# A two-layer decoder trunk on one core: the SSM preparation cut into pieces, and the first output block placed among the last attention products

## The chip, the cores and the metric

The program runs on one core of one Trainium2 chip. A core has TensorE (PE: matmuls; PEld is its weight load), VectorE (DVE), ScalarE (ACT), GpSimd (POOL) and SyncE (SP, which here issues most DMAs). The metric is the device time of one execution in microseconds (us), and lower is better. Several runs are timed and the median is taken.

## The reference, cut to what matters

Two layers work on a residual of 1024 tokens by 1024 channels. Layer 0 mixes tokens by attention, layer 1 by a state-space recurrence (S5) beside a short convolution; each mixer is followed by an MLP (1024 to 4096 to 1024, squared ReLU) and a gated per-layer embedding (PLE).

```
for i in range(2):
    hn = rms_norm(h, norm_mix[i])
    y = attention_mixer(hn, ...) if i == 0 else recurrent_conv_mixer(hn, ...)   # each ends in y @ w_out
    h = h + y
    h = h + square(relu(rms_norm(h, norm_mlp[i]) @ w_mlp_in[i])) @ w_mlp_out[i]
    h = h + (p[i] @ w_ple_proj[i]) * sigmoid(rms_norm(h, norm_ple[i]) @ w_ple_gate[i])
return rms_norm(h, norm_final)
```

The attention has 8 groups of 128 channels (4 differential heads, 4 pairs of dilated-window heads), so `y` is 8 blocks of 128 channels. The recurrence of layer 1 needs tables that depend on weights alone (powers of the complex decay, rotations, small products): they can be made at any time before layer 1, and this is called the preparation here.

## The kernel before, in words

**Products.** Activations lie transposed, channels on partitions, tokens (1024, two halves of 512) along the free dimension. Every f32 operand is split into a high part (ACT, `hi`, L76) and a low part (DVE, `lo`, L79, or `wtile`, L89), and a product is three matmuls in a row, high x high, low x high, high x low (`mm3`, L95 to L97). A weight block of 128 output channels is one `wtile`: a 512 KB DMA on SP's queue into `wr` (2 buffers), ACT's `wh`, then `wl` by DVE (by POOL during the attention); `wh` and `wl` have 3 buffers. `blocks` (L273 on) runs the output blocks of a projection: the first two or three share a loop over the 8 input blocks, then each block has 48 matmuls, two times 8 x 3, and a result bank is emptied by `out`.

**Order.** TensorE executes in the order in which the program is written. On the other engines the instructions are put in order by a planner at build time: of those that it takes to be ready it issues the one that the program names first. Tiles wait for the release of the tile whose memory or buffer they take over.

**Attention** (`at_run`, L1655 on). The order on TensorE is written by a small model of the engines with four lanes: `s` (scores), `t` (transposes of the weights), `pv` (products with v) and `u` (scaling and output). A list `fill` of projections (q, k, v and part of the PLE) is fed in between, in steps of three matmuls, while a lane has nothing due. When one list entry nears its end, `prime` starts the next one, which issues its weight DMAs. `s` has 128 tasks, four for each of 8 x 4 steps (group i, quarter of the queries). The last list entry is the q and k projection of group 7. `y_out` (L2022 on) writes each quarter of a `y` block to HBM.

**Output projection of layer 0** (`out_proj`, L328 on) loads the 8 blocks of `y` from HBM into the memory of the attention's input (`y_load`, L322), in order of SP's queue, and runs `blocks` with the first two output blocks together.

**MLP up of layer 0** (`mlp_up_plain`, L356 on). 32 blocks; `out(m, n, ps)` scales a bank, and after the second half applies ReLU and square and for odd m combines and stores (`z_out`). The preparation `s5_prep` is a generator that `out` advances at nine blocks (m = 1, 5, 9, ..., 27): the first time all of the tables and the first of 8 quads, then one quad (`s5_quad`) each time; a quad's part on TensorE (`later`) is emitted at the next call. The tiles of `out` lie in a pool `cu` on the left side of SBUF, ahead of the preparation's pool. The MLP down (`mlp_down`) then opens its pool `dn` on the left, over `cu`.

**Output projection of layer 1** (`out_proj_halves`, L409 on) runs the left token half, then the right half; while the right half's blocks m = 1 and 2 run, `out` also normalizes and splits four blocks each of the left half for the MLP that follows.

Of the kernel before, what the change touches and what calls it, by code (L numbers as in the profile page):

```python
# [65 lines left out]
class Trunk:  # L66
# [95 lines left out]
    def run(self):  # L162
        tc, nc, A = self.tc, self.nc, self.A
        pool = tc.tile_pool
        with pool(name="w", bufs=1, side=LEFT) as self.wp, \
# [11 lines left out]
            for l in range(2):  # L177
                if l == 0:
                    self.attention(xp)
                with pool(name=f"md{l}", bufs=6, space=PSUM, reuse_waits="tile") as self.mx, ExitStack() as rs:  # L180
# [4 lines left out]
                    if l == 0:  # L185
                        with pool(name=f"xu{l}", bufs=1, side=RIGHT, reuse_waits="tile") as xu:
                            hp = hs.enter_context(pool(name=f"h{l}", bufs=1, side=RIGHT, reuse_waits="tile"))
                            sp = self.ss.enter_context(pool(name=f"st{l}", bufs=1, side=RIGHT, reuse_waits="tile"))
                            xs, st = self.out_proj(l, xp, hp, xu, sp)
                            nxt.close()  # L190
                            with pool(name=f"cu{l}", bufs=1, side=LEFT, reuse_waits="tile") as cu:
                                first = self.mlp_up_plain(l, xs, st, cu, xu, hs)
# [135 lines left out]
    def out_proj(self, l, xp, hp, xq, sp):  # L328
        nc, A = self.nc, self.A
        ws = []  # L330
        if l:
            ws = [self.wtile(A["w_out"][l * KB + j]) for j in range(3)]
            order = [4, 5, 6, 7, 0, 1, 2, 3]
        else:
            order = list(range(KB))
            self.ys = {}
        ys = self.ys
        for k in order:
            if k not in ys:
                self.y_load(xp, k)  # L340
# [12 lines left out]
        self.blocks(A["w_out"][l * KB : (l + 1) * KB], ys, KB, order, out, 2 if l == 0 else 3, None if l == 0 else 4, ws)  # L353
        return xs, st

    def mlp_up_plain(self, l, xs, st, cu, xu, hs):  # L356
# [5 lines left out]
        def out(m, n, ps):  # L362
            if not r:
                r.append(self.rstd_full(st, xu, cu))
                self.ss.close()
                hs.close()
            s = slice(n * H, n * H + H)
# [14 lines left out]
        with self.tc.tile_pool(name=f"s0{l}", bufs=1, side=LEFT, reuse_waits="tile") as self.s0:  # L382
# [26 lines left out]
    def out_proj_halves(self, l, xp, hp, sp, xa, X):  # L409
# [35 lines left out]
        for s in (lt, rt):  # L445
            for m in range(3 if s is lt else 0, KB):
# [514 lines left out]
    def s5_prep(self):  # L961
# [4 lines left out]
        with tc.tile_pool(name="prep", bufs=1, side=LEFT, reuse_waits="tile") as pr:  # L966
# [16 lines left out]
            self.pexp(dt, ld, tmp)  # L983
            x = tmp()
            v.tensor_tensor(x, lr, dt, ALU.mult)
            self.pexp(mag, x, tmp)
            x = tmp()
            v.tensor_tensor(x, li, dt, ALU.mult)
            self.sincos(sn, cs, x, tmp)

# [19 lines left out]
            for t in range(8):  # L1010
                for j in range(2):
                    nc.scalar.copy(rv[j][:, t * G : (t + 1) * G], w(j, 7 - t))

# [14 lines left out]
            v.tensor_tensor(ci, ci, den, ALU.mult)  # L1028

# [16 lines left out]
            pend = None  # L1046
            for q in range(8):
                if pend:
# [3 lines left out]
            pend()  # L1052
# [11 lines left out]
    def s5_quad(self, q, pr, pw, rv, cr, ci, rot, sgn, nsgn):  # L1064
# [21 lines left out]

        def outer(out, tab, nt, X1, X2):
# [9 lines left out]
        outer(Gt, rv, 8, bb1, bb2)  # L1097
        CA = big("CA", 576)
        outer(CA, pw, 9, C1, C2)
        ca4 = CA.rearrange("p (g t c) -> p g t c", g=4, c=16)  # L1100
        cc = big("cc")
        nc.scalar.copy(cc.rearrange("p (g t c) -> p g t c", g=4, c=16), ca4[:, :, 1:9, :])
        self.spill(pr, q, 4, cc)

# [4 lines left out]
        for j in range(7):  # L1109
# [9 lines left out]
            v.tensor_tensor(s3[:, :, hi], s3[:, :, hi], m, ALU.add)  # L1119
        v.tensor_scalar(st, st, sgn, None, ALU.mult)  # L1120
# [3 lines left out]
        def later():  # L1124
            ps = self.bank()
            for g in range(4):
                nc.tensor.transpose(ps[:, g * P : g * P + P], Gt[:, g * P : g * P + P], self.ident)
            self.spill(pr, q, 2, ps)
            kp = self.bank()
            for g in range(4):  # L1130
                nc.tensor.matmul(kp[0:16, g * P : g * P + P], bb1[:, g * 16 : g * 16 + 16], ca4[:, g, 0:8, :], start=True, stop=True)
            M = big("M")
            v.memset(M, 0.0)
            kt = big("kt")[0:16]
            nc.scalar.copy(kt, kp[0:16, :])
            k4 = kt.rearrange("p (g t c) -> p g t c", g=4, c=16)
            di = pr.tile([16, 64], F32, name="di", tag="di", bufs=1)
            v.tensor_tensor(g4(di), self.ident[0:16, 0:16].unsqueeze(1).to_broadcast([16, 4, 16]),
                            self.s5_dT[:, gs].unsqueeze(2).to_broadcast([16, 4, 16]), ALU.mult)
            v.tensor_tensor(k4[:, :, 0, :], k4[:, :, 0, :], g4(di), ALU.add)  # L1140
            m4 = M.rearrange("p (g t c) -> p g t c", g=4, c=16)
            for t in range(8):
                nc.sync.dma_start(m4[t * 16 : t * 16 + 16, :, t:8, :], k4[:, :, 0 : 8 - t, :])
            self.spill(pr, q, 0, M)
        return later
# [290 lines left out]
    def attention(self, xp):  # L1436
        tc, nc, A = self.tc, self.nc, self.A
        with tc.tile_pool(name="at", bufs=1, side=RIGHT) as self.ap, \
             tc.tile_pool(name="sps", bufs=3, space=PSUM) as self.sp, \
             tc.tile_pool(name="tps", bufs=1, space=PSUM) as self.tp:  # L1440
            self.o2, self.on = None, 0
            v0 = self.at_start(xp)
# [131 lines left out]


# [79 lines left out]
    def at_run(self, v0):  # L1655
# [3 lines left out]
        fill = [("v", 0)]  # L1659
        for i in range(1, 8):  # L1660
            fill += [("qk", i)] + ([("v", i // 2)] if i % 2 == 0 else []) + late.get(i, [])
        made = {"qk": self.qk, "v": self.vproj, "pp": self.ple_proj}
# [4 lines left out]
        def may(f):  # L1667
            if f[0] == "v":
# [3 lines left out]
        def prime(n):  # L1672

            if n < len(fill) and n not in gens and (fill[n][0] != "pp" or may(fill[n])):
# [347 lines left out]
    def y_out(self, st, y):  # L2022
# [6 lines left out]
        s = slice(qp * 256, qp * 256 + 256)  # L2029
        nc.sync.dma_start(self.y_d[i][0][:, s], yh.bitcast(F32))  # L2030
# [76 lines left out]
```

## Time and profile before

| | |
|---|---|
| median of 3 runs | 2575.11 us (2574.72 to 2578.71) |
| profiled execution, its own time | 2579.28 us |
| its span, first to last instruction | 2577.5 us |
| mean granted TensorE clock | 0.985 of full |
| PE busy | 2486.7 us (96%) |
| DVE busy | 1726.0 us (67%) |
| ACT busy | 1082.6 us (42%) |
| POOL busy | 131.3 us (5%) |

A profile is one execution. Times in its rows are counted from the span's start. In a timeline row the numbers are start, length, engine, line, operation, output <- inputs, shape and count, and in brackets how long the engine was idle before it and what ended that. The granted clock has two levels, full and half (2.4 and 1.2 GHz).

### The profile page before, as it was taken

Reading aid. Unit: us, or ns where it says so; the run is one execution under the profiler, and the core shown is the slowest. Engines: PE = TensorE matmul, PEld = TensorE weight load, DVE = VectorE, ACT = ScalarE, POOL = GpSimd, SP = SyncE. Lnnn points to the kernel's source line nnn. Section 1 sums busy time; section 2 is a strip of 40 time slices with the busy share of each in tenths; the row PEclk is TensorE's granted clock in tenths of the full one; section 3 lists DMA queues with packets and bytes.
Section 4 is the critical chain, followed back from the end, with each engine's and each line's share of the span. In section 5 each row is a group of like instructions: output and inputs, shape, how many; then the busy total and the mean of one; then the engine's idle time right before and its main releaser. Section 6 shows DMA issues by size and latency. Waiting matters only on the chain.

```text
span 2577.5 us, 33019 instructions
## 1 busy us (share of the span) xinstructions
PE 2486.7 (96%) x12104; PEld 2057.1 (80%) x12104; DVE 1726.0 (67%) x3189; ACT 1082.6 (42%) x1615; POOL 131.3 (5%) x128
## 2 busy tenths in 40 slices
PE   8999999979899999899999999999899999999998
PEld 6888898968687877688887897887688887888877
DVE  6776756554766776356776768665786664568776
ACT  5554555542333333343344432333554444333445
POOL 1111111000000000000000000000000000000000
PEclk9999999989999999999999999999999999999999
DMA  5443524264254555677853656354353447677552
GB/s 175 111 131 97 150 63 118 61 198 154 85 180 164 197 190 193 270 239 242 282 191 134 212 171 194 131 187 132 139 196 135 152 170 297 235 243 280 202 183 97
DMA packets 184754, 449.82 MB, mean 175 GB/s; under 512 B 24848, under 2 KB 56848, under 8 KB 184592
## 3 DMA queue, kind: packets, MB, share of 16 engines
q1 hardware_dynamic: 155904, 371.94, 43.8%
q0 software_dynamic: 12800, 46.14, 4.6%
q10 hardware_dynamic: 15888, 29.63, 3.1%
q8 instruction: 95, 1.56, 0.3%
q14 instruction: 67, 0.55, 0.1%
HBM read 297.55 MB, written 123.73 MB: 163 GB/s over the span
## 4 chain that ended last, share of the span: by engine, by line
PE 85%; DVE 8%; ACT 2%; issue 2%; DMA 1%; SPq 0%; DVEq 0%; ACTq 0%
PE mm L95 26%; PE mm L97 26%; PE mm L96 26%; PE tp L1927 2%; PE S L1894 1%; PE S L1895 1%; PE o L1952 1%; PE o L1951 1%; DVE zl L79 1%; DVE p L1897 1%; PE S L2019 1%; DVE wl L89 0%; DVE h L465 0%; DVE tl L79 0%; DVE p L1916 0%
## 5 line engine op out<-in xcount | busy, mean ns | idle before, releaser
L97 PE MATMUL mm<-xh,wl 128*128 128x512 f32 (+1 forms) x1504 | 583.9, 388 | 13.4 <-DVE st L1108 8.7
L95 PE MATMUL mm<-xh,wh 128*128 128x512 f32 (+1 forms) x1504 | 589.9, 392 | 0.3 <-ACT wh L76 0.3
L96 PE MATMUL mm<-xl,wh 128*128 128x512 f32 (+1 forms) x1504 | 580.8, 386 | 1.6 <-DVE xl L155 1.6
L95 PE MATMUL mm<-zh,wh 128*128 128x512 f32 x880 | 350.2, 398 | 8.5 <-ACT zh L76 8.5
L96 PE MATMUL mm<-zl,wh 128*128 128x512 f32 x880 | 350.1, 398 | 1.7 <-DVE zl L79 1.7
L97 PE MATMUL mm<-zh,wl 128*128 128x512 f32 x880 | 349.8, 397 | 0.0
L97 PEld LDWEIGHTS mm<-xh,wl 128*128 128x128 f32 x1504 | 284.5, 189 | 78.2 <-DVE st L1108 9.1
L96 PEld LDWEIGHTS mm<-xl,wh 128*128 128x128 f32 x1504 | 284.7, 189 | 61.4 <-DVE xl L155 2.0
L95 PEld LDWEIGHTS mm<-xh,wh 128*128 128x128 f32 x1504 | 284.6, 189 | 59.8 <-ACT sph L76 1.5
L76 ACT ACTIVATE wh<-wr 128x1024 fp32r<-128x1024 f32 (+1 forms) x137 | 143.8, 1052 | 446.1 <-PE mm L96 356.1
L95 PEld LDWEIGHTS mm<-zh,wh 128*128 128x128 f32 x880 | 166.4, 189 | 49.9 <-ACT zh L76 9.3
L96 PEld LDWEIGHTS mm<-zl,wh 128*128 128x128 f32 x880 | 166.4, 189 | 43.0 <-DVE zl L79 2.5
L97 PEld LDWEIGHTS mm<-zh,wl 128*128 128x128 f32 x880 | 166.3, 189 | 40.5
L76 ACT ACTIVATE wh<-raw 128x1024 fp32r<-128x1024 f32 x78 | 82.7, 1060 | 239.9 <-issue 117.0
L79 DVE TENSOR_TENSOR wl<-raw,wh 128x1024 fp32r<-128x1024 f32 x78 | 95.4, 1223 | 100.3 <-ACT wh L76 100.2
L89 DVE TENSOR_TENSOR wl<-wr,wh 128x1024 fp32r<-128x1024 f32 x98 | 119.6, 1222 | 59.6 <-ACT wh L76 59.3
L1902 ACT ACTIVATE p<-p,m 128x128 f32<-128x128 f32 (+7 forms) x128 | 99.1, 774 | 96.6 <-DVE m L1897 95.5
L79 DVE TENSOR_TENSOR zl<-zr,zh 128x1024 fp32r<-128x1024 f32 x110 | 134.1, 1219 | 2.4 <-ACT zh L76 2.2
L76 ACT ACTIVATE zh<-zr 128x1024 fp32r<-128x1024 f32 x110 | 115.0, 1045 | 0.7 <-DMA zr<-oa 0.7
L95 PE MATMUL mm<-wh,xh 128*128 128x256 f32 x384 | 112.6, 293 | 2.1 <-DVE v L1651 1.4
L97 PE MATMUL mm<-wh,xl 128*128 128x256 f32 x384 | 109.7, 286 | 0.0
L96 PE MATMUL mm<-wl,xh 128*128 128x256 f32 x384 | 109.6, 285 | 0.0
(680 smaller groups left out, 4476.2 us busy)
## 6 DMA issues: line engine op xcount, KB each, us to landing
raw<-w_m SPq DMA_DIRECT2D x158, 512.0 KB, 5.8
wr<-w_m SPq DMA_DIRECT2D x69, 512.0 KB, 4.1
ot<-tt POOLq DMA_DIRECT2D x64, 512.0 KB, 5.0
zr<-ot SPq DMA_DIRECT2D x64, 512.0 KB, 4.9
ob<-z ACTq DMA_DIRECT2D x32, 512.0 KB, 4.6
zr<-ob SPq DMA_DIRECT2D x32, 512.0 KB, 4.2
s<-s SPq DMA_DIRECT2D x64, 256.0 KB, 5.0
wr<-w_out SPq DMA_DIRECT2D x24, 512.0 KB, 3.5
```

Of the source, the lines that this page charges most:

```text
L76: self.nc.scalar.activation(out, in_, AF.Copy, scale=scale)
L79: self.nc.vector.tensor_tensor(out, full, hi.bitcast(F32), ALU.subtract)
L89: self.weng.tensor_tensor(l, raw, h.bitcast(F32), ALU.subtract)
L95: mm(ps, L[0], R[0], start=first, stop=False)
L96: mm(ps, L[0], R[1], start=False, stop=False)
L97: mm(ps, L[1], R[0], start=False, stop=last)
L1894: nc.tensor.matmul(S, qh, qk["k"][c][:, k], start=True, stop=False)
L1895: nc.tensor.matmul(S, ql, qk["k"][c][:, k], start=False, stop=True)
L1897: nc.vector.tensor_tensor_reduce(pt[:, k], S, self.tab[:, T - w + k.start : T - w + k.stop], -0.125, m, ALU.add, ALU.min, m2)
L1902: nc.scalar.activation(pt[:, :w], pt[:, :w], AF.Exp, bias=m, scale=-1.0, accum_out=den)
L1927: nc.tensor.transpose(tps[:, off + n * P : off + n * P + P], maps[j][:, kb * P : kb * P + P], self.ident)
L1951: nc.tensor.matmul(oq, vv, th[:, q], start=first, stop=False)
```

## The change: what it does

1. **Preparation in pieces.** `s5_prep` and `s5_quad` yield 6 times in the tables and 9 times in each quad, and `later` becomes a straight continuation of its quad. `out` of `mlp_up_plain` advances the generator once after the first half and twice after the second half of every block from m = 1, so three pieces per block.
2. **Pools of the MLP up.** `cu` is opened on the right side of SBUF, where the output projection's `h` and statistics lay, after these are closed. The four temporaries of the norm go into the pool `s0` on the left.
3. **First output block as filler.** A new list entry `("op",)` follows the q and k projection of group 7. `op_start` loads the block's weights and `y` blocks 0 to 5, then gives 12 steps of three matmuls into two banks. It may be primed once `y_out` was emitted for groups 0 to 5; its steps may run once 10 or fewer `s` tasks are left, and only when no lane is due. `out_proj` loads `y` 6 and 7, runs output blocks 1 and 2 over `y` 0 to 5, then all three blocks over `y` 6 and `y` 7, empties six banks and goes on with blocks 3 to 7.
4. **Layer 1.** The normalizing and splitting of the left half is spread over the right half's m = 1 to 4, two blocks each.

```diff
@@ out_proj
+        for k in (6, 7):
+            self.y_load(xp, k)
...
+        self.bn = 2
+        ws = [self.op[0]] + [self.wtile(src[m]) for m in (1, 2)]
+        jobs = [(m, n, self.op[1][n] if m == 0 else self.bank()) for m in range(3) for n in range(2)]
+        for part in (range(6), (6,), (7,)):
+            for m, n, b in jobs:
+                if m or part[0]:
+                    for k in part:
+                        self.mm3(b, self.cols(ws[m])(k), [y[:, n * H : n * H + H] for y in ys[k]], k == 0, k == KB - 1)
+        for m, n, b in jobs:
+            out(m, n, b)
+        self.blocks(src[3:], ys, KB - 3, list(range(KB)), lambda m, n, b: out(m + 3, n, b), 1)
@@ mlp_up_plain
-                r.append(self.rstd_full(st, xu, cu))
+                r.append(self.rstd_full(st, xu, self.s0))
                 self.ss.close()
                 hs.close()
+                r.append(cs.enter_context(self.tc.tile_pool(name=f"cu{l}", bufs=1, side=RIGHT, reuse_waits="tile")))
...
-                if m in (1, 5, 9, 12, 16, 19, 22, 25, 27):
+            if m:
+                for _ in range(1 + n):
                     next(prep, None)
@@ out_proj_halves
-                if s is rt and m in (1, 2):
-                    for k in range(m * 4 - 4, m * 4):
+                if s is rt and m in (1, 2, 3, 4):
+                    for k in range(m * 2 - 2, m * 2):
                         self.norm_half(l, h, st, k, lt)
-                        X[m, k % 4] = self.split(h[k][:, lt], xa, (f"x{k}h", f"x{k}l"), 1)
+                        X[k // 4 + 1, k % 4] = self.split(h[k][:, lt], xa, (f"x{k}h", f"x{k}l"), 1)
@@ s5_prep
-                pend = self.s5_quad(q, pr, pw, rv, cr, ci, rot, sgn, nsgn)
-                yield
-            pend()
+                yield from self.s5_quad(q, pr, pw, rv, cr, ci, rot, sgn, nsgn)
@@ new
+    def op_start(self):
+        self.ys = {}
+        w = self.wtile(self.A["w_out"][0])
+        for k in range(6):
+            self.y_load(self.xp0, k)
+        yield 0.0
+        self.op = (w, [])
+        for n in range(2):
+            s = slice(n * H, n * H + H)
+            self.op[1].append(self.bank())
+            for k in range(6):
+                self.mm3(self.op[1][n], self.cols(w)(k), [y[:, s] for y in self.ys[k]], k == 0, False)
+                yield 0.65
@@ at_run
+        fill.append(("op",))
...
+            if f[0] == "op":
+                return all((i, q) in self.ydone for i in range(6) for q in range(4))
...
-                if not may(fill[n]):
+                if not may(fill[n]) or fill[n][0] == "op" and len(lanes["s"]) > 10:
                     return None
...
-            if (lane is None or t["fill"] < t["main"] - 2.0) and fill_step():
+            op = state["n"] < len(fill) and fill[state["n"]][0] == "op"
+            if (lane is None or t["fill"] < t["main"] - 2.0 and not op) and fill_step():
```

## Rows read from the trace of the kernel before

**Rows 1.** Waits of PE, whole span: engine, line, releaser: us, times, longest.
```profile
PE mm L97 <- DVE st L1108: 8.7, 1, 8.7
...
PE mm L95 <- ACT zh L76: 8.5, 2, 8.2
...
PE mm L97 <- DVE wl L89: 4.7, 2, 2.7
```

**Rows 2.** Stretches: from:to, us, busy and count of each engine; PEclk, DMA share, GB/s.
```profile
519.00:571.30 52.30, 37.96 (x218) 33.50 (x217) 33.88 (x89) 30.76 (x69) 0.00 (x0) 0.84 0.59 192
...
520.00:523.50 3.50, 0.30 (x1) 0.19 (x1) 1.92 (x2) 0.70 (x2) 0.00 (x0) 0.89 1.03 234
...
575.00:655.00 80.00, 80.00 (x343) 64.32 (x342) 33.17 (x34) 21.42 (x21) 0.00 (x0) 1.00 0.43 157
...
696.50:705.20 8.70, 0.01 (x1) 0.01 (x1) 8.70 (x29) 2.98 (x4) 1.67 (x2) 0.71 0.69 253
705.20:710.50 5.30, 5.30 (x13) 4.14 (x14) 4.57 (x31) 1.14 (x2) 0.00 (x0) 0.50 0.88 272
...
740.00:1020.00 280.00, 280.00 (x1243) 223.79 (x1242) 194.48 (x576) 93.27 (x110) 17.41 (x24) 1.00 0.55 186
...
1050.65:1058.84 8.19, 0.01 (x1) 0.01 (x1) 1.04 (x1) 2.08 (x2) 0.25 (x1) 0.78 0.87 299
1058.84:1065.20 6.36, 5.78 (x13) 4.21 (x14) 4.01 (x5) 3.18 (x4) 0.00 (x0) 0.50 1.00 379
1065.50:1071.90 6.40, 6.40 (x29) 5.16 (x28) 4.27 (x4) 2.76 (x3) 0.00 (x0) 1.00 1.02 414
...
1785.90:1789.10 3.20, 3.20 (x8) 2.53 (x9) 1.66 (x2) 0.00 (x0) 0.00 (x0) 0.50 0.71 207
```

**Rows 3.** Timeline of ACT, MLP up of layer 0, around block 3.
```profile
682.32 1.06 ACT L76 ACTIVATE wh<-wr 128x1024 fp32r<-128x1024 f32 x1 [1.59 <-PE mm L96]
```

**Rows 4.** Timeline of DVE in the same stretch.
```profile
694.26 0.70 DVE L1094 TENSOR_TENSOR Gt<-rv,bb 128x512 f32<-128x512 f32 x1
...
703.92 1.22 DVE L89 TENSOR_TENSOR wl<-wr,wh 128x1024 fp32r<-128x1024 f32 x1
```

**Rows 5.** Waits of SP's queue, 1000 to 1070 us (MLP down of layer 0 begins).
```profile
SPq L668 <- DMA ob<-z: 26.0, 1, 26.0
```

**Rows 6.** Timeline of PE, the same place of layer 1.
```profile
2159.24 0.50 PE L95 MATMUL mm<-zh,wh 128*128 128x512 f32 x1 [0.29 <-ACT zh L76]
2160.83 0.50 PE L96 MATMUL mm<-zl,wh 128*128 128x512 f32 x1 [1.09 <-DVE zl L79]
```

**Rows 7.** Timeline of DVE, right half of layer 1's output projection.
```profile
1779.60 0.75 DVE L465 SCALAR_TENSOR_TENSOR h<-h,gains,rstd 128x512 f32<-128x512 f32 x1
...
1784.00 0.69 DVE L79 TENSOR_TENSOR x7l<-h,x7h 128x512 fp32r<-128x512 f32 x1
1784.60 1.22 DVE L89 TENSOR_TENSOR wl<-wr,wh 128x1024 fp32r<-128x1024 f32 x1
```

**Rows 8.** Timeline of SP's queue, end of the attention.
```profile
514.37 0.33 SPq L325 DMA_DIRECT2D xh<-y0h  x1
...
520.87 0.51 SPq L1601 DMA_DIRECT2D q<-zh  x1
...
525.28 0.59 SPq L1602 DMA_DIRECT2D ql<-zl  x1
525.92 0.59 SPq L325 DMA_DIRECT2D xl<-y0l  x1
```

**Rows 9.** DMAs issued from 505 to 575 us: count, KB each, median us to landing.
```profile
ql<-zl SPq DMA_DIRECT2D x8, 128.0 KB, 4.0
...
xh<-y3h SPq DMA_DIRECT2D x1, 512.0 KB, 8.1
```

**Rows 10.** Timeline of PE, attention group 7.
```profile
530.99 0.48 PE L1894 MATMUL S<-k,q 128*128 128x512 f32 x1
...
554.05 0.55 PE L1951 MATMUL o<-th,v 128*128 128x256 f32 x1 [3.12 <-DVE y L2000]
```

More of the change, by code (lines that the diff above doesn't have):

```diff
@@ L190, in run @@
                             nxt.close()
-                            with pool(name=f"cu{l}", bufs=1, side=LEFT, reuse_waits="tile") as cu:
-                                first = self.mlp_up_plain(l, xs, st, cu, xu, hs)
+                            first = self.mlp_up_plain(l, xs, st, xu, hs)
                     else:
@@ L329, in out_proj @@
         nc, A = self.nc, self.A
[L330 to L336, printed above, removed]
+        src = A["w_out"][l * KB : (l + 1) * KB]
         ys = self.ys
-        for k in order:
-            if k not in ys:
-                self.y_load(xp, k)
+        for k in (6, 7):
+            self.y_load(xp, k)
         h, xs, st = {}, [], self.stats_new((sp, "acc", 1), (sp, "sq", 1) if l == 0 else (xp, "rstd", 1))
@@ L352, in out, with mlp_up_plain @@
                 self.stat_block(st, h[m])
-        self.blocks(A["w_out"][l * KB : (l + 1) * KB], ys, KB, order, out, 2 if l == 0 else 3, None if l == 0 else 4, ws)
+        self.bn = 2
[9 more added lines that the diff above has]
+        self.blocks(src[3:], ys, KB - 3, list(range(KB)), lambda m, n, b: out(m + 3, n, b), 1)
         return xs, st
-    def mlp_up_plain(self, l, xs, st, cu, xu, hs):
+    def mlp_up_plain(self, l, xs, st, xu, hs):
         nc, A = self.nc, self.A
@@ L378, in out @@
                     self.z_out(m // 2, z.pop(m - 1), z.pop(m), cu)
-                if m in (1, 5, 9, 12, 16, 19, 22, 25, 27):
+            if m:
+                for _ in range(1 + n):
                     next(prep, None)
-        with self.tc.tile_pool(name=f"s0{l}", bufs=1, side=LEFT, reuse_waits="tile") as self.s0:
+        with self.tc.tile_pool(name=f"s0{l}", bufs=1, side=LEFT, reuse_waits="tile") as self.s0, ExitStack() as cs:
             for t in ("sf", "sh", "sl"):
@@ L983, in s5_prep @@
             self.pexp(dt, ld, tmp)
+            yield
             x = tmp()
@@ L986, in s5_prep @@
             self.pexp(mag, x, tmp)
+            yield
             x = tmp()
@@ L989, in s5_prep @@
             self.sincos(sn, cs, x, tmp)
+            yield
             pw = [keep(f"pw{j}", (P, 9 * G)) for j in range(2)]
@@ L1012, in s5_prep @@
                     nc.scalar.copy(rv[j][:, t * G : (t + 1) * G], w(j, 7 - t))
+            yield
             den, nr, cr, ci, y = tmp(), tmp(), keep("cr"), keep("ci"), tmp()
@@ L1028, in s5_prep @@
             v.tensor_tensor(ci, ci, den, ALU.mult)
+            yield
             self.dec = self.cp.tile([P, G], F32, name="dec")
@@ L1085, in s5_quad @@
         v.tensor_tensor(bb2, bb2, raw, ALU.subtract)
+        yield
         def outer(out, tab, nt, X1, X2):
@@ L1097, in s5_quad @@
         outer(Gt, rv, 8, bb1, bb2)
+        yield
         CA = big("CA", 576)
         outer(CA, pw, 9, C1, C2)
+        yield
         ca4 = CA.rearrange("p (g t c) -> p g t c", g=4, c=16)
@@ L1103, in s5_quad @@
         self.spill(pr, q, 4, cc)
+        yield
         ct, st = big("ct"), big("st")
@@ L1119, in s5_quad @@
             v.tensor_tensor(s3[:, :, hi], s3[:, :, hi], m, ALU.add)
+            if j in (2, 4):
+                yield
         v.tensor_scalar(st, st, sgn, None, ALU.mult)
@@ L1122, in s5_quad @@
         nc.sync.dma_start(self.s5_d[q][7], st)
[L1124 to L1144, printed above, removed]
@@ L1145, in s5_quad @@
-        return later
+        yield
+        ps = self.bank()
+        for g in range(4):
+            nc.tensor.transpose(ps[:, g * P : g * P + P], Gt[:, g * P : g * P + P], self.ident)
+        self.spill(pr, q, 2, ps)
+        kp = self.bank()
+        for g in range(4):
+            nc.tensor.matmul(kp[0:16, g * P : g * P + P], bb1[:, g * 16 : g * 16 + 16], ca4[:, g, 0:8, :], start=True, stop=True)
+        yield
+        M = big("M")
+        v.memset(M, 0.0)
+        kt = big("kt")[0:16]
@@ new lines, in s5_quad @@
+        nc.scalar.copy(kt, kp[0:16, :])
+        k4 = kt.rearrange("p (g t c) -> p g t c", g=4, c=16)
+        di = pr.tile([16, 64], F32, name="di", tag="di", bufs=1)
+        v.tensor_tensor(g4(di), self.ident[0:16, 0:16].unsqueeze(1).to_broadcast([16, 4, 16]),
+                        self.s5_dT[:, gs].unsqueeze(2).to_broadcast([16, 4, 16]), ALU.mult)
+        v.tensor_tensor(k4[:, :, 0, :], k4[:, :, 0, :], g4(di), ALU.add)
+        m4 = M.rearrange("p (g t c) -> p g t c", g=4, c=16)
+        for t in range(8):
+            nc.sync.dma_start(m4[t * 16 : t * 16 + 16, :, t:8, :], k4[:, :, 0 : 8 - t, :])
@@ L1147, in recurrent @@
+        self.spill(pr, q, 0, M)
+        yield
     def recurrent(self, xp):
@@ L1441, in attention @@
             self.o2, self.on = None, 0
+            self.xp0 = xp
             v0 = self.at_start(xp)
@@ L1659, in at_run @@
         fill = [("v", 0)]
+        self.ydone = set()
         for i in range(1, 8):
             fill += [("qk", i)] + ([("v", i // 2)] if i % 2 == 0 else []) + late.get(i, [])
-        made = {"qk": self.qk, "v": self.vproj, "pp": self.ple_proj}
+        fill.append(("op",))
+        made = {"op": self.op_start, "qk": self.qk, "v": self.vproj, "pp": self.ple_proj}
         gens, done = {0: v0}, {("qk", 0)}
@@ L1672, in prime @@
         def prime(n):
-            if n < len(fill) and n not in gens and (fill[n][0] != "pp" or may(fill[n])):
+            if n < len(fill) and n not in gens and (fill[n][0] not in ("pp", "op") or may(fill[n])):
                 gens[n] = made[fill[n][0]](*fill[n][1:4])
@@ L2029, in y_out @@
         s = slice(qp * 256, qp * 256 + 256)
+        self.ydone.add((i, qp))
         nc.sync.dma_start(self.y_d[i][0][:, s], yh.bitcast(F32))
```

5 lines of the change are left out of this document (2 added, 3 removed).

## The prediction

> **What bounds the kernel now.** I read the page's busy shares first: PE is busy for 96% of the span, so a gain can only come from the 4% in which it stands still and from stretches in which its clock is at half. The waits of PE come next [rows 1]. Three single waits stand out, and each lies in code that the change touches: 8.7 us behind the preparation's DVE work, 8.2 us for the second operand of layer 0's MLP down, and two waits for a weight's low part of which the longer is 2.7 us. The stretches [rows 2] then show what follows each: the granted clock drops to 0.50 just after the wait, and in that time PE executes about half as many matmuls. The last place is the tail of the attention: from 519.0 us, when the last projection ends, to 571.3 us, when the output projection begins, PE is busy for 37.96 of 52.30 us, at a mean clock of 0.84 [rows 2].
>
> A matmul of 512 columns at full clock costs 80.00 / 343 = 0.233 us [rows 2]. All sums below are in that unit and against the profiled execution's 2579.28 us; the median of the runs shown is 4.17 us lower, and I carry the difference over unchanged.
>
> **Part A, preparation in pieces.** PE idles for 8.7 us until 705.2, and then executes 13 matmuls in 5.30 us where full clock would need 13 x 0.233 = 3.03; so the half clock costs 2.3 us and the place 11.0. What it waits for is block 3's `wl`. Its high part was started at 682.32 [rows 3], but DVE came to the low part only at 703.92 [rows 4]: in between it worked on the tables and on the first quad (its `Gt` is at 694.26), which the program names ahead of block 3's weight. After the change only the six table pieces come ahead of that weight; the first quad's pieces begin in `out(3, 0)`, behind it. The tables have the two lead blocks' time (96 matmuls, 22.4 us) in which DVE has almost nothing else. So of the 21.6 us between the two rows the quad's part goes, some 8 us, and the weight should be ready before PE needs it, which is 11.2 us after block 2 began. Bounds: the whole 11.0 comes back, or half of it, if the norm's own DVE work and the rest of the rotations still stand ahead. I take 10.5, near the first, because the weight has a slack of a whole block. From then on DVE's total is unchanged: 194.5 of 280 us while the quads run [rows 2], or 7.8 us in a block of 11.2, with no PE idle time at all in that stretch. The smaller pieces fit into the same room, so I cost the rest at nothing; what covers it is the 3.4 us that DVE has free in a block.
>
> **Part B, pools.** The 8.2 us wait is a chain over SP: the load of the next weights of `mlp_down` waited for 26.0 us on the store of a `z` tile [rows 5], because `dn` lies on the memory of `cu`, whose last tiles are stored when the last block is done. With `cu` on the right, `dn` lies on `s0` and on the preparation's tiles, which are done some four blocks (45 us) earlier. Layer 1 already has this arrangement, and its first steps idle for 0.29 + 1.09 = 1.38 us [rows 6] with no drop of the clock in the stretch. Before: 8.19 idle, then 6.36 - 5.78 = 0.58 idle in the next stretch, then 13 matmuls in 5.78 us of busy time (13 x 0.233 = 3.03), so 2.75 lost to the clock: 11.5 in all. Minus layer 1's 1.38: a gain of 10.1. Bounds 0 (another late tile underneath) and 11.5. Nothing is added on PE. The norm's temporaries wait for the output projection's last matmul as before, since their memory is the same region.
>
> **Part C, layer 1.** The low part of block 3's weight came at 1784.60, directly behind the last of the eight splits [rows 7]; PE idled for 2.7 us and then ran 8 matmuls in 3.20 us (1.87 at full clock), so 1.3 more: 4.1. A split costs DVE 0.75 + 0.69 = 1.4 us. Four fewer in blocks 1 and 2 free 5.7 us ahead of that weight, more than the 2.7 by which it was late, so I take the whole 4.1. In blocks 3 and 4 DVE then has 2 x 1.4 for the splits beside 0.69 + 0.69 + 1.22 for the block itself: 5.4 us in the 5.6 that 24 matmuls take. It fits barely; what waits for the splits is the MLP, four blocks later. Bounds 0 and 4.1.
>
> **Part D, filler.** 36 matmuls, 8.4 us, move from behind the attention into its tail, where PE has 14.3 us of idle time. Were this all, up to 8.4 would come back; I would count on 6.4, because the gaps are not all where the order's model sees them (3.12 us at 554.05 [rows 10] is one real gap). But the step also issues 12 loads of `y`, 512 KB each, on SP. `prime` emits them at the first step of the last q block, so they stand in the program ahead of that block's q copies, which are emitted at its end. Before, only `y0h` came ahead, and the copies of the second token half were issued from 520.87 to 525.28, with the other `y` loads behind them from 525.92 [rows 8]. After, eleven loads go first. At 234 GB/s and a DMA share of 1.03 the engines are full until 523.5; 11 x 0.524 MB at the 414 GB/s that a stretch of large loads shows [rows 2] is 13.9 us, and the eight copies (1.05 MB at 234 GB/s) take 4.5: they land at about 541, not 529 (525.28 + 4.0 [rows 8, 9]). That landing grows with what is in front is seen in the sixth load of a row: 8.1 us [rows 9]. The first scores that need the second half start at 530.99 [rows 10], and PE executes in order, so all that stands behind them waits, up to 10 us. The 36 matmuls partly fill this new wait and partly the old gaps, so their 8.4 us stay hidden. Sum: 10 - 8.4, and about 0.6 back because ACT catches up meanwhile: 1 us lost. Bounds: 8.4 gained, 8 lost (the wait stays and nothing is hidden). In `out_proj` itself the number of matmuls is unchanged; `y` 7 is needed 72 + 18 matmuls (21 us) after the attention, before it was needed after 84.
>
> The Trainium skill weighs in on this queue: "DMA: Bandwidth & Descriptors", section "Queues, rings and completion order", says that each SDMA engine consumes one issuer's descriptors in ring order, but that a later one may finish its write before an earlier one. Its first half stands with the growing landing times and with the 1 us lost; its second half would favour the first rival. No row here shows a small copy overtaking large loads.
>
> **Sum.** -10.5 - 10.1 - 4.1 + 1.0 = -23.7: 2555.6 for a profiled execution, and 2575.11 - 23.7 = 2551.4 for the median.
>
> **The rivals.**
> 1. The `y` loads do not hold up the copies (they are issued behind them, or overtaken), and the filler brings its 6.4. For it: the tail has the idle time. Against: the order of names and the full DMA engines. D turns from +1.0 to -6.4: 2544.0.
> 2. DVE still comes late to block 3's weight, or to one of the next, as the tables' rotations and the norm fill the time: half of A is lost, 5.5: 2556.9 with all else as forecast. For it: 20 us of delay before. Against: the first quad is gone from ahead of it.
> 3. B brings nothing, because `dn`'s tiles still take over a late tile: 2561.5. Against it stands layer 1, where the same arrangement runs [rows 6].
> 4. The other side, slower: three pieces in every block put DVE work ahead of each next weight, and the wait of block 3 comes back in small in all of the 24 or so blocks with quads. It needs a block's DVE work to exceed its 11.2 us, 7.8 now; from there each further us per block costs 24 us, and 1.2 over (one `wl`) costs 29: 2580. Against: 69% of DVE in that stretch, PE never idle in it [rows 2].
> 5. The filler does not run in the tail at all, because the model never has an empty moment; then the loads still hold up the copies: D is +8, 2558.
>
> **How the numbers follow.** Forecast 0.52, rivals in order 0.25, 0.08, 0.05, 0.05, 0.05. The likeliest's own range is 2545 to 2558; with the first three rivals and the fifth the range is 2539 to 2564 (rival 1 with a better tail at the one end, rival 3 with some of rival 2 at the other). A measurement of this kernel can tell about 0.2% (5.2 us) from no change. All cases but the fourth are faster than 2569.9 unless two failures meet; I give 0.89 to faster, 0.06 to same, 0.05 to slower.
>
> **What would show it.** A: PE's wait behind the preparation is gone or under 2 us, and the clock stays at 1.00 near 700 us. B: the loads of `mlp_down` are issued before the last block ends, and PE idles for under 2 us there. C: no wait for `wl` in the right half. D: on SP's queue the `y` loads stand ahead of the last eight q copies, and PE waits some 5 to 10 us for a DMA in front of group 7's third quarter. The prediction is wrong if PE waits for `wl` or for the quads' transposes within blocks 4 to 27, if a new wait appears at the six banks of `out_proj`, or if the last q copies land as early as before.

## The result, and the profile after

The changed kernel takes 2558.0 us (median of 4 runs, 2556.8 to 2562.5), the kernel before in the same measurement 2576.91: a ratio of 0.993, 95% interval 0.9912 to 0.9947. The forecast was 2551.4, with a range of 2539 to 2564. The profiled execution took 2557.15 us where that of before took 2579.28, so 22.1 us less against the 23.7 forecast; the medians differ by 18.9. Single slow runs stand in no ratio or range below.

PE's waits of the changed kernel, whole span (columns as in [rows 1]):

```profile
PE S L1929 <- DMA q<-zh: 8.5, 1, 8.5
...
PE S L1930 <- DMA ql<-zl: 5.8, 5, 1.9
PE o L1986 <- DVE y L2035: 5.0, 5, 1.8
...
PE mm L95 <- ACT sh L76: 4.4, 1, 4.4
```

All three waits of [rows 1] are gone from the places they had (the 2.0 us left of the third group is its shorter member, in a stage that the change doesn't touch). At the top stands a new one of 8.5 us for a DMA of q. The stretches show the same (columns as in [rows 2]; the attention's tail, a part of it, the lead of MLP up, the blocks with quads, the start of MLP down, layer 1's right half):

```profile
517.40:583.40 66.00, 45.59 (x253) 38.82 (x253) 34.05 (x89) 30.82 (x69) 0.00 (x0) 0.84 0.47 151
535.00:545.30 10.30, 4.36 (x11) 3.23 (x12) 1.06 (x4) 0.92 (x2) 0.00 (x0) 0.50 1.03 289
683.00:720.00 37.00, 37.00 (x160) 29.80 (x159) 35.49 (x130) 18.51 (x30) 3.13 (x4) 1.00 0.49 171
700.00:980.00 280.00, 280.00 (x1239) 223.97 (x1237) 211.10 (x645) 95.47 (x113) 19.12 (x26) 1.00 0.58 198
1037.00:1047.00 10.00, 8.94 (x38) 6.69 (x37) 7.38 (x9) 7.92 (x8) 1.45 (x2) 1.00 0.53 181
1755.00:1795.00 40.00, 40.00 (x173) 32.15 (x172) 29.31 (x39) 17.75 (x25) 3.25 (x6) 1.00 0.46 151
```

The third, fourth and sixth rows have PE busy without a gap at clock 1.00, the fifth has one gap of 1.06 us and clock 1.00. Only the tail got worse: 66.00 us with 20.4 idle, where [rows 2] has 52.30 with 14.3 idle, and it holds 36 matmuls, 8.4 us at full clock, that used to come later.

To compare kernels whose attention doesn't end at the same moment, I cut the span at landmarks on PE: (a) the last matmul of the last projection in the attention, (b) the first sum of squares in layer 0's MLP (`mm<-rs_a`), (c) the first matmul of MLP down (`mm<-sh,wh`), (d) the first with the weight as moving operand behind it (`mm<-wh,xh`), (e) layer 1's first `mm<-gg`, (f) the first `mm<-p0h` behind layer 1's output projection. Part D lies between a and b, A between b and c, B between c and d, C between e and f. All kernels that were run, each from its one profile; the ratio is to runs of the kernel before on the same chip (its median there 2576.4 to 2577.9):

| kernel | profiled, us | ratio [95%] | a | a to b | b to c | c to d | e to f |
|---|---|---|---|---|---|---|---|
| before | 2579.28 | 1 | 518.86 | 164.89 | 361.12 | 421.58 | 134.54 |
| after | 2557.15 | 0.9930 [0.9912, 0.9947] | 517.02 | 170.41 | 349.77 | 411.04 | 130.08 |
| e1_no_filler | 2557.37 | 0.9912 [0.9894, 0.9930] | 521.65 | 164.76 | 349.78 | 411.30 | 130.08 |
| e2_loads_behind | 2553.56 | 0.9901 [0.9884, 0.9919] | 520.81 | 163.49 | 349.77 | 409.75 | 130.08 |
| e3_pools_left | 2567.96 | 0.9965 [0.9952, 0.9978] | 518.09 | 170.12 | 349.78 | 420.93 | 130.08 |
| e4_lumps | 2567.37 | 0.9959 [0.9944, 0.9975] | 520.66 | 170.24 | 357.21 | 409.76 | 130.08 |
| e5_layer1_old | 2557.06 | 0.9934 [0.9917, 0.9950] | 516.73 | 167.72 | 349.78 | 409.74 | 134.63 |
| e6_tables_first | 2557.76 | 0.9926 [0.9909, 0.9942] | 517.09 | 171.29 | 349.78 | 409.74 | 130.08 |
| e7_later_fill | 2546.01 | 0.9873 [0.9858, 0.9887] | 519.65 | 155.56 | 349.79 | 411.29 | 130.08 |
| e8_loads_alone | 2567.62 | 0.9957 [0.9941, 0.9974] | 521.43 | 177.12 | 349.78 | 409.75 | 130.08 |
| e9_loads_pool | 2556.72 | 0.9919 [0.9904, 0.9934] | 520.10 | 166.85 | 349.77 | 409.74 | 130.08 |
| e10_fill_8 | 2553.88 | 0.9900 [0.9883, 0.9916] | 519.51 | 164.52 | 349.78 | 409.73 | 130.08 |

From before to after: a -1.8, D +5.5, A -11.4, B -10.5, C -4.5, and +0.5 in all the rest, together -22.2 of the span. The stretches that hold A and C repeat to 0.02 us, c to d to 1.6. The stretch a to b is looser: the five kernels with D as in the change (after, e3 to e6) have 167.7 to 171.3, so a difference of 3 us between two single profiles there can be chance. And a itself wanders from 516.7 to 521.7 among kernels whose attention is the same up to there, so a single profile's total says little about 5 us, and a stretch says much.

SP's queue shows, on the left, the start of each issue; first the tail, where the order is the one that part D forecast, and last the first load of MLP down:

```profile
518.88 0.46 SPq L1632 DMA_DIRECT2D ql<-zl  x1
519.38 0.58 SPq L324 DMA_DIRECT2D xl<-y0l  x1
...
526.90 0.32 SPq L324 DMA_DIRECT2D xl<-y5l  x1
528.23 0.47 SPq L1631 DMA_DIRECT2D q<-zh  x1
...
537.98 0.46 SPq L1632 DMA_DIRECT2D ql<-zl  x1
...
1017.53 0.38 SPq L673 DMA_DIRECT2D raw<-w_m  x1
```

And PE's timeline shows what it did meanwhile. Its first row is (a) and its last (b); the rows from 528.34 to 529.50 are the first two filler steps, 583.41 is the first matmul of the output projection behind the attention:

```profile
517.02 0.40 PE L97 MATMUL mm<-xh,wl 128*128 128x512 f32 x1
...
528.34 0.39 PE L95 MATMUL mm<-xh,wh 128*128 128x512 f32 x1
...
529.50 0.39 PE L97 MATMUL mm<-xh,wl 128*128 128x512 f32 x1
...
539.27 0.77 PE L1929 MATMUL S<-k,q 128*128 128x512 f32 x1 [8.52 <-DMA q<-zh]
541.71 0.77 PE L1930 MATMUL S<-k,ql 128*128 128x512 f32 x1 [1.67 <-DMA ql<-zl]
...
583.41 0.48 PE L95 MATMUL mm<-xh,wh 128*128 128x512 f32 x1
...
687.43 0.39 PE L118 MATMUL mm<-rs_a,ones 128*128 128x512 f32 x1
```

Two of the twelve steps, 528.34 to 529.50, stand ahead of the wait; ten come after it. A matmul at 539.27 takes 0.77 us where 0.39 to 0.48 is usual: the granted clock is 0.50 from 535.0 to 545.3, as the second row of the stretches has it.

### The profile page after: what moved, and what is told of

Read it like the earlier page. It is cut to its first block, busy times and chain, and to the rows that moved or that the text cites. A ratio compares the mean times of both kernels' runs of the same rounds, so it can differ in the third digit from the quotient of the medians.

```text
span 2555.3 us, 33046 instructions
## 1 busy us (share of the span) xinstructions
PE 2476.9 (97%) x12104; PEld 2048.4 (80%) x12104; DVE 1725.1 (68%) x3188; ACT 1082.2 (42%) x1615; POOL 133.8 (5%) x129
## 4 chain that ended last, share of the span: by engine, by line
PE 86%; DVE 7%; ACT 2%; DMA 2%; issue 1%; DVEq 0%; SPq 0%; ACTq 0%
PE mm L95 26%; PE mm L97 26%; PE mm L96 26%; PE tp L1962 2%; PE S L1930 1%; PE S L1929 1%; PE o L1987 1%; PE o L1986 1%; DVE zl L79 1%; PE S L2054 1%; DVE p L1932 0%; DMA xl<-y4l 0%; DVE tl L79 0%; DVE p L1951 0%; ACT p L1937 0%
```

## The experiments

**e1_no_filler** leaves part D out: the output projection is that of before, A, B and C stay.

```
-        fill.append(("op",))
...
 def out_proj(...): as in the kernel before
```

> The changed kernel without its part D: no output block as filler, the old output projection. Theory (the y loads named ahead of the last q copies made PE wait 10.2 us, and the hidden 8.4 us of matmuls pay for less than that): PE's waits of 8.5 and 1.7 us for a DMA in group 7 go, the 36 matmuls come back behind the attention, and the time falls by about 5 us, to 2552 in a profile and 2553 in the median. Rival (the filler pays in spite of the wait, and the missing gain of the whole lies elsewhere): the time rises by 3 to 6 us, to 2561 to 2564.

Measured: 0.9912; a to b is 164.76, that of before (164.89), and D's price by this pair is 170.41 - 164.76 = 5.65 us. With the other four kernels that have D as in the change it is 3.0 to 6.5. The medians lie 3.7 us apart (2554.31 and 2558.0), and the two intervals of the ratios overlap; the profiled execution did not get shorter, as (a) came 4.6 us later in it. So the stretch decides, and in it D by itself costs time in all five.

**e2_loads_behind** keeps the filler, but names the early `y` loads behind the last q copies.

```
-                    if fill[n][0] != "qk" or state["k"] > 24:
+                    if (... as before ...) and fill[n + 1 : n + 2] != [("op",)]:
                         prime(n + 1)
```

> The changed kernel with the filler primed only when the last q block is done, so that the y loads are named behind the last q copies. Theory (order on SP's queue): the copies are issued from about 519 and land 8 to 10 us earlier, the 8.5 us wait in front of group 7's third quarter goes, PE waits 3 to 4 us for y 0 and 1 instead, and the time falls by 4 to 8 us, to 2549 to 2553 in a profile. Rival (the loads and the copies share the DMA engines whatever their order): the waits add up to about 10 us again and the time stays at 2557.

Measured: 0.9901; a to b 163.49. No score of the second half of q waits any more (1.0 us is left ahead of the group's first score), so the loads were the cause of the 8.5. But the filler now brought only 1.3 us (164.76 - 163.49), no more than the spread of this stretch, where 36 matmuls are 8.4. PE's timeline shows why:

```profile
529.52 0.40 PE L95 MATMUL mm<-xh,wh 128*128 128x512 f32 x1
531.20 0.50 PE L96 MATMUL mm<-xl,wh 128*128 128x512 f32 x1 [1.28 <-DMA xl<-y0l]
532.57 0.49 PE L95 MATMUL mm<-xh,wh 128*128 128x512 f32 x1 [0.64 <-DMA xh<-y1h]
534.28 0.50 PE L96 MATMUL mm<-xl,wh 128*128 128x512 f32 x1 [1.22 <-DMA xl<-y1l]
...
544.51 0.50 PE L96 MATMUL mm<-xl,wh 128*128 128x512 f32 x1 [0.78 <-DMA xl<-y5l]
```

The first step comes before its `y` has landed, and as PE executes in order the attention's scores stand behind it. From 529.5 to 544.5 PE goes at the pace of the loads; its waits for `y` add up to 5.0 us. The wait had changed its name.

**e3_pools_left** puts part B back: `cu` on the left again.

```
-                            first = self.mlp_up_plain(l, xs, st, xu, hs)
+                            with pool(name=f"cu{l}", bufs=1, side=LEFT, reuse_waits="tile") as cu:
+                                first = self.mlp_up_plain(l, xs, st, cu, xu, hs)
```

> The changed kernel with the MLP up's tiles back on the left, ahead of the preparation (part B undone). Theory (the second operand waited for the release of these tiles): SP's weight load waits over 20 us for the store of a z tile, PE idles about 8 us at the start of the MLP down of layer 0, and the time rises by 10 us, to 2567 in a profile. Rival (the wait came from the preparation's last lump, which is in pieces now): no such wait, 2557.

Measured: 0.9965; c to d is 420.93, 9.9 over the change's and 11.2 over the 409.74 of others. PE waits again for the second operand, the first fence, and SP's queue waits again for the store of `z`, the second:

```profile
PE mm L95 <- ACT zh L76: 8.1, 2, 7.8
```
```profile
SPq L672 <- DMA ob<-z: 25.9, 1, 25.9
```

In the change the first load of MLP down leaves at 1017.53, 19.7 us ahead of (c); here it leaves 6.3 us after (c), as its row of SP's timeline shows:

```profile
1044.33 0.33 SPq L672 DMA_DIRECT2D raw<-w_m  x1
```

**e4_lumps** puts part A back: eight lumps of preparation, one at each of nine blocks, the first with the tables.

```
-            if m:
-                for _ in range(1 + n):
-                    next(prep, None)
+            if n and m in (1, 5, 9, 12, 16, 19, 22, 25, 27):
+                next(prep, None)
```

> The changed kernel with the preparation in the old lumps at the old nine blocks (part A undone). Theory (tables and first quad are named ahead of block 3's weight): PE waits about 8 us for block 3's low part again with half the clock behind it, and the time rises by 11 us, to 2568 in a profile. Rival (the wait came from where the preparation's memory lay, which part B moved): no wait, 2557.

Measured: 0.9959; b to c 357.21, 7.4 over the change. DVE's timeline has block 3's `wl` 16 us behind the first quad's `Gt`, and PE waits 5.5 us for it (the second fence):

```profile
691.66 0.69 DVE L1098 TENSOR_TENSOR Gt<-rv,bb 128x512 f32<-128x512 f32 x1
...
707.89 1.22 DVE L89 TENSOR_TENSOR wl<-wr,wh 128x1024 fp32r<-128x1024 f32 x1
```
```profile
PE mm L97 <- DVE wl L89: 7.5, 2, 5.5
```

The wait is 3.2 us shorter than the 8.7 of [rows 1], because PE itself comes later: with D in place (b) is 690.90 - 683.75 = 7.15 us later than before, and `wl` only 707.89 - 703.92 = 3.97 later [rows 4]. So the price of the lumps depends on what stands ahead of them. That the profiled total still rose by 10 us, close to the 11 expected, is chance: (a) was 3.6 us later in it.

**e5_layer1_old** puts part C back.

```
-                if s is rt and m in (1, 2, 3, 4):
-                    for k in range(m * 2 - 2, m * 2):
+                if s is rt and m in (1, 2):
+                    for k in range(m * 4 - 4, m * 4):
```

> The changed kernel with part C alone put back: the norms and splits of layer 1's left half come four by four in two blocks of the right half, as before. Theory (C gave its price): TensorE waits 2.7 us again for the low half of a weight in layer 1's right half and runs 3.4 us at 1.2 GHz behind it; the time is 4.1 to 4.5 us longer than the changed kernel's, about 2561.5 to 2562. Rival (C's gain was an accident of when the stage began): no wait there, 2557 to 2558.

Measured: 0.9934; e to f 134.63 against 130.08, so 4.55, and PE's wait of 2.7 us for `wl` is back. The profiled total is not longer than the change's, as (b) came 3.0 us earlier in it; the median is, by 2.5 us. PE's waits have the row of before:

```profile
PE mm L97 <- DVE wl L89: 4.7, 2, 2.7
```

**e6_tables_first** asks what in A did it, the smallness of the pieces or the order. It has the old lumps, but a piece of its own for the tables, so that the first quad is named two blocks later (the edit is shown against e4_lumps).

```
             pend = None
+            yield
             for q in range(8):
...
-            if n and m in (1, 5, 9, 12, 16, 19, 22, 25, 27):
+            if n and m in (1, 3, 6, 9, 12, 16, 19, 22, 25, 27):
```

> The changed kernel with the recurrence's preparation in its eight old lumps, one in every third block, except that the tables end with a piece of their own, so the first lump of a quad is issued two blocks later and block 3's weight stands on VectorE ahead of it. Theory (A's gain is only that this weight is named ahead of the first quad): no wait of TensorE for a weight in layer 0's MLP, the time of the changed kernel, 2556 to 2559, and from the first sum matmul of that stage to the first product of mlp_down 349 to 351 us. Rival (it is the smallness of the pieces that did it, a lump of a quad is late for some weight wherever it stands): a wait of 3 to 7 us and half the clock behind it, 2563 to 2567, and 354 to 358 us in that stretch.

Measured: 0.9926; b to c 349.78, that of the change, and no wait of PE for a weight in that stage. DVE does block 3's `wl` ahead of `Gt`:

```profile
689.15 1.22 DVE L89 TENSOR_TENSOR wl<-wr,wh 128x1024 fp32r<-128x1024 f32 x1
691.89 0.68 DVE L1099 TENSOR_TENSOR Gt<-rv,bb 128x512 f32<-128x512 f32 x1
```

The whole of A is the order of one weight and one quad. Cutting the lumps small is worth nothing here.

**e7_later_fill** is e2_loads_behind with the filler's steps held back until 6 score tasks are left, so that each block of `y` lands ahead of the step that reads it.

```
-                if not may(fill[n]) or fill[n][0] == "op" and len(lanes["s"]) > 10:
+                if not may(fill[n]) or fill[n][0] == "op" and len(lanes["s"]) > 6:
```

> The changed kernel with the y loads named behind the last q copies (as in e2_loads_behind), and the filler steps not let in until 6 softmax units are left in place of 10, so that y has landed when they come. Theory (the last waits of the tail are y's loads, 4 to 7 us in e2_loads_behind): no wait for y there, 2 to 3 us below e2_loads_behind: 2549 to 2551. Rival (the tail is bound by VectorE's chain, and what the fillers don't cover early they lengthen later): the same as e2_loads_behind or up to 2 us above, 2552 to 2555.

Measured: 0.9873, 2543.44 us (median of 4, 2541.78 to 2546.01): 14.6 us below the change and 5.6 below the lower end of what the theory gave. The direction was right and the size was not. a to b is 155.56, 9.2 below e1. The first step starts 3 us later than in e2, and no step waits for `y` by more than 0.1 us. Not all of `y` is there at that moment (`y5l` lands at 542.97); each block comes in time for its own step. The first step, and the tail from the last projection to the output projection's first matmul:

```profile
532.50 0.40 PE L95 MATMUL mm<-xh,wh 128*128 128x512 f32 x1
```
```profile
520.00:571.20 51.20, 42.09 (x253) 36.37 (x253) 33.63 (x89) 30.49 (x69) 0.00 (x0) 0.93 0.56 192
```

It holds the 36 matmuls and is still 1.1 us shorter than [rows 2] has it without them. Idle time fell from 14.3 to 9.1 us, and the mean clock rose from 0.84 to 0.93: worked out from these means, PE spends about 7 us of it at half speed, where before it spent 17. That second gain is what no sum of mine held. Against e2, whose tail of 59.3 us has 13.9 idle, 4.8 us of idle time are gone, about the 5.0 that e2 waits for `y`; the other 3.3 are busy time.

**e8_loads_alone** takes the other half of D: the loads where the change has them, and the twelve steps behind the attention.

```
-                if not may(fill[n]) or fill[n][0] == "op" and len(lanes["s"]) > 10:
+                if not may(fill[n]) or fill[n][0] == "op" and any(lanes.values()):
```

> The changed kernel with the y loads where the change puts them, ahead of the last q copies, and none of the twelve filler steps among the attention's last products: they run behind the last of them. Theory (in the part D the loads cost about 8 us of wait and half clock, and the fillers give back 4 to 6): first S of the left over q copies waits 8 to 10 us as in the changed kernel, and the time is 2 to 6 us above the changed kernel's, 2559 to 2564. Rival (the fillers give nothing, D's cost is the loads' alone): 2557 to 2558. Other rival (the fillers themselves crowd the tail, and the wait is absorbed): below 2556.

Measured: 0.9957, 2565.58 us, 1.6 above the theory's 2559 to 2564; a to b 177.12. The tail:

```profile
521.80:586.10 64.30, 38.93 (x217) 34.03 (x217) 34.06 (x89) 30.66 (x69) 0.00 (x0) 0.79 0.47 155
```

Without steps the loads make the tail 64.30 - 52.30 = 12.0 us longer; in the table it is 177.12 - 164.76 = 12.4. Its waits in that stretch:

```profile
PE S L1929 <- DMA q<-zh: 9.2, 1, 9.2
PE o L1986 <- DVE y L2035: 7.5, 3, 3.6
...
PE S L1930 <- DMA ql<-zl: 3.8, 2, 2.1
```

With the steps (the change) the tail is 66.00 for 36 matmuls more, so they hide 8.4 - 1.7 = 6.7 us by this pair. By the spread of the five kernels with the steps it could be 6 to 9; that the steps help is clear of it, as all five are at least 5.8 us below e8.

**e9_loads_pool** issues the twelve early loads on GpSimd's queue.

```
-            self.y_load(self.xp0, k)
+            self.y_load(self.xp0, k, self.nc.gpsimd)
```

> The changed kernel, except that the twelve early y loads go out on GpSimd's DMA queue and no longer on SyncE's, so the last q copies have nothing ahead of them in their own queue. Theory (the copies wait because they stand behind the loads in one queue): the wait for the first S over the second half of q falls from 8.5 us to 1 to 4 us, the stretch from the first S of the last group to the first sum matmul of layer 0's MLP comes down from 167.4 us to 158 to 162 us, and the time is 2549 to 2553 us. Rival (the 16 DMA engines are full whichever queue it is, about 410 GB/s in these 15 us, and the copies get their turn late all the same): the wait stays at 6 us or more and the time at 2555 to 2558.

Measured: 0.9919, 2556.55 us; a to b 166.85, 3.6 less than the change but only 0.9 below the lowest of the five kernels with the same D, and 2.1 more than e1. The wait that the theory names is gone: the first score over the second half of q waits for no copy (the row below), and its second matmul 1.0 us for `ql`. In its place the copies of the first half come late: PE waits 4.0 us for q ahead of the group's first score and then 5.3 and 1.6 for `ql`. All waits for copies are 11.9 us, where the change has 14.7, and two waits for `y5`, 2.4 us, are new. From the group's first score, at 524.53, to (b) it is 162.42, at the edge of the theory's range, and the time is the rival's.

```profile
539.96 0.47 PE L1929 MATMUL S<-k,q 128*128 128x512 f32 x1
```

The DMAs issued from 500 to 550 us (count, KB, median us to landing):

```profile
q<-zh SPq DMA_DIRECT2D x8, 128.0 KB, 9.9
ql<-zl SPq DMA_DIRECT2D x8, 128.0 KB, 10.9
...
xl<-y5l POOLq DMA_DIRECT2D x1, 512.0 KB, 19.6
```

Both got slower, the copies from [rows 9]'s 4.0 to 10.9 and the last load to 19.6 us. So the second queue doesn't set the copies free: the two queues share engines that are full (in the stretch from 539 to 547 us at a share of 1.03). The Trainium skill, "DMA: Bandwidth & Descriptors", section "Queues, rings and completion order", says that each engine takes turns between the queues that have work for it; these landing times agree. The issues themselves need no coupling between the queues: on either one an issue follows the landing of the transfer eight places earlier in the same queue (on SP a copy at 522.23 after 522.16, on GpSimd's queue `y5h` at 526.62 after 526.11). So here slower landing also makes later issue, and how much of the copies' delay is the one and how much the other is not told apart.

**e10_fill_8** is e7 with 8 in place of 6.

> e7_later_fill with the filler steps let in at 8 softmax units left in place of 6: between e2_loads_behind (10) and e7_later_fill (6). Theory (what decides is only whether y has landed when the first step comes): if at 8 it has, the same as e7_later_fill, 2542 to 2545, and no wait for a y load; if it hasn't, waits for y loads of 1 to 4 us and half the clock behind them, 2545 to 2550. Rival (the waits for y in e2_loads_behind are not its loss, and it is the steps' place among the last softmax units that counts): more than 2550.

Measured: 0.9900, the time of e2 (0.9901). The first step starts at 529.57 and waits 1.2 us for `y0l`, as in e2: between 10 and 8 the model has the same empty moment. It is a repeat of e2 and places the edge between 8 and 6. Its 2552.12 us lies above the 2545 to 2550 expected for late `y`, in the rival's range of more than 2550, so this run does not refute the rival; that e2's waits for `y` account for the idle time between it and e7 speaks against it.

## Why the prediction was right, and where not

**Part A** was right in mechanism and size: 11.35 us against 10.5. DVE starts `wl` of block 3 at 688.20, ahead of `Gt`, as said:

```profile
688.20 1.22 DVE L89 TENSOR_TENSOR wl<-wr,wh 128x1024 fp32r<-128x1024 f32 x1
...
690.94 0.68 DVE L1102 TENSOR_TENSOR Gt<-rv,bb 128x512 f32<-128x512 f32 x1
```

e6 shows that this order is the cause. The 11.35 is the price in the kernel before; put back into the changed kernel, the lumps cost 7.4 (e4), since PE then reaches the place later. That the smaller pieces cost nothing also held: from (b) to (c) DVE is busy for 242.6 us after and 242.9 before, and PE has no idle time there after. (The 211.10 of 280 us, against 194.5 in [rows 2], is no more work: its stretch begins nearer to (b).) Rivals 2 and 4 are refuted with it.

**Part B** was right: 10.54 against 10.1, by e3 9.9 to 11.2. The residue is one wait of 1.04 us, less than the 1.38 taken from layer 1 [rows 6]. Rival 3 is refuted.

**Part C** was right: 4.46 against 4.1 (its own terms, 2.7 and 1.3, add to 4.0), by e5 4.55.

**Part D** is the term that was mis-sized: +1.0 forecast, +5.5 measured, +5.65 against e1 and 3.0 to 6.5 with the other kernels that have it. Its mechanism stands: the order on SP's queue and the wait for q came as described, and the last copy landed at 542.7, where the prediction's terms add to 541.9. Both of its terms were off, and to the same side.

The loads were put at 10 less the 0.6 that I took ACT to give back; e8 has 12.0. Three things make the difference. From 530.99 to the 541.9 of its own terms are 10.9 us and not 10, and 10.9 is what PE waits in e8, 9.2 for q and then 1.7 for `ql`, which the second matmul of the same score needs. The half clock that follows a wait was priced in A, B and C and put at nothing here; PE is busy for 38.93 - 37.96 = 1.0 us longer in e8's tail. And the 0.6 did not come: the waits for results of DVE are 9.4 us in this tail as in that of before.

The filler was put at 8.4 hidden; it hid 6.7. The step that failed is "the 36 matmuls partly fill this new wait and partly the old gaps, so their 8.4 us stay hidden". Only 6 of 36 stand ahead of the wait, since the rest has its turn in PE's order behind the waiting score, and the wait is shorter by only 0.7 us than e8's (8.52 for 9.22). Behind it the steps did fill gaps (the gap at `o` like the 3.12 us of [rows 10] is 3.62 in e8 and 1.80 in the change), but 20.4 us stay idle, for e8's 25.4. So 5.0 of the 6.7 are idle time, and 1.7 are less time at half clock, although the first six matmuls behind the wait still run at half clock (535.0 to 545.3). The two errors, 2.6 + 1.7, are the 4.3 between 1.0 and the tail's own 5.3 (66.00 - 52.30 - 8.4). That D costs more than forecast holds for all five kernels with it; the split into 2.6 and 1.7 rests on one profile of e8, and 1.7 is within the spread of these kernels.

**Rival 1** was the better kernel, not the one built. Its variant with the copies overtaking the loads did not occur: in the change the last load landed at 537.96 and the copies behind it from 538.47 on. With the loads behind the copies the rival gave 2544.0, and e7, which also holds the steps back, has 2543.4. That the two agree so well is partly luck, as D is -9.2 there against the rival's -6.4. Loads behind the copies alone (e2) don't reach it, so the rival as written lacked a condition: each block of `y` must be in SBUF when its step comes. **Rival 5** had D's cost of 8 without the filler; e8 has 12. Its total, 2558, is the median measured, but by chance, for the steps did run in the tail, from 528.34 on.

**The sum** came nearer than its terms, by luck: D cost 4.5 more than forecast, while A, B and C gave 1.7 more and the attention ended 1.8 earlier, which no part of the change explains; other kernels with the same instructions up to there differ by more. The median is 6.6 above the forecast: 1.6 from the profiled difference (22.1 for 23.7), 1.8 because the kernel before has 2576.91 in the joint measurement where the forecast started from 2575.11, and 3.2 because the two profiled executions lie on opposite sides of their medians (before 2.4 above, after 0.85 below).

## What to carry to other kernels

A filler for idle time is worth its matmuls only if its data has landed when its turn comes and if its loads stand behind the transfers that the critical chain still waits for; test the two by themselves, loads without work and work with late loads, before crediting the sum. On an engine that executes in order a filler placed behind a waiting instruction cannot fill that wait. And when a late weight costs time, look first for the one piece of work named ahead of it: here moving that behind the weight gave all that cutting the work small gave.

## What was not expected of the hardware

**At most eight transfers of a queue are under way, so issue is paced by landing.** Before, SP issued the last eight q copies 0.55 to 0.70 us apart (520.87 to 525.28, [rows 8]). With the loads ahead it took 528.23 to 537.98, 1.4 us apart on average, and the last `y` loads 1.2 to 1.3 apart; a 512 KB load at the 414 GB/s of [rows 2] takes 1.27. SP's waits from 505 to 560 us name an older transfer's landing, that of the transfer eight places earlier in the queue:

```profile
SPq L1632 <- DMA xl<-y5l: 1.6, 1, 1.6
...
SPq L1632 <- DMA xh<-y0h: 1.1, 1, 1.1
```

`y0l`, for example, was issued at 519.38 and landed at 524.32, and the load eight places behind it was issued at 524.34. In the whole trace of the change none of the 1111 issues on SP's queue starts before the transfer eight places earlier has landed. With eight under way the loads' landing time rose along the row (the DMAs issued from 495 to 545 us); eight times 1.27 is 10.2:

```profile
xl<-y0l SPq DMA_DIRECT2D x1, 512.0 KB, 4.9
...
xl<-y5l SPq DMA_DIRECT2D x1, 512.0 KB, 11.1
```

In the trace the transfers of SP's queue use eight semaphores, and the load that waited for `y0l` signals the same one as `y0l`. That points to the program's bookkeeping and not to the chip as what sets the number; it was not tried with another one.

**A filled tail ran at a higher clock.** In e7 the same attention work with 36 matmuls in its gaps ran at a mean of 0.93 where it ran at 0.84, and the tail was shorter with them than without. During each of PE's long waits the granted clock fell to 0.50 and stayed there behind it (in the change from 535.0, in the wait of 8.5 us, to 545.3; in [rows 2] 0.71 in the mean of the wait of 8.7 us and 0.50 in the 5.3 behind it), and where the steps closed the gaps it stood at half for less of the time.
